# Own work tiles for the odd early stages of an RWKV layer, a new order of the stages, and two operations moved from VectorE to ScalarE

## The chip, the cores and the metric

The kernel runs on one core of one Trainium2 chip. The metric is the device time of one execution in microseconds; the time of a kernel is the median of several executions. The engines are named as the profile names them: PE is TensorE (matmuls; PEld is its weight load), DVE is VectorE, ACT is ScalarE, POOL is GpSimd, and SP is the engine whose queue issues nearly all DMA transfers.

## The reference

Two layers on a sequence of 512 tokens with 1024 features, all in float32. Layer 0 mixes tokens with RWKV-7, layer 1 with a spatial gating unit; a SwiGLU block with 2816 hidden features follows each. Every sub-layer is `x + RMSNorm(f(RMSNorm(x)))`. The part that matters here is the front of RWKV-7:

```python
xs = x[None] + xx[None] * mix[:, None, None, :]          # six mixed inputs
r, k, v = jnp.einsum('cbtd,cde->cbte', xs[:3], w_rkv)
w_raw = (w0 + jnp.tanh(xw @ w1) @ w2)
w_log = -jax.nn.softplus(-w_raw) - 0.5
decay = jnp.exp(-jnp.exp(w_log))
a = jax.nn.sigmoid(a0 + (xa @ a1) @ a2)                  # the rate
g = jax.nn.sigmoid(xg @ g1) @ g2
kk = heads(k * k_k)
kk = kk / jnp.maximum(jnp.sqrt(jnp.sum(kk * kk, axis=-1, keepdims=True)), 1e-12)
k = k * (1.0 + (a - 1.0) * k_a)
y = _rwkv7_scan(r_h, decay, k_h, v_h, -kk, kk * a_h)     # then group norm, bonus, gate, w_o
```

The scan updates a 64 x 64 state in each of 16 heads, token by token.

## The kernel before

**Tiling.** Features lie on the 128 partitions, and the 512 tokens along a row. A float32 product of full size is three matmuls of split operands (`mm3`, lines 156 to 158): each operand is split into a rounded part (`hi`, written by ScalarE, line 131) and the rest (`lo`, by VectorE, line 132). A weight comes by `weight` (line 138): a DMA into one of two `wraw` buffers, then the two halves of the split.

**Stages of the RWKV layer.** The 16 heads are worked in four groups of four heads (256 features, two slices `q` of 128), numbered b = 0 to 3. A list by hand, `PLAN` (line 33), gives the order in which the stages are written into the program:

- `P`b, `kr_proj`: the projections of k and r for the group, each copied out of PSUM by ScalarE (line 528).
- `E`b, `early`: everything for the group that works on features. From two small products it makes tanh values `tw` (decay) and `ta` (rate); a running sum `cum` of `tw` in chunks of 64 tokens; the two exponentials `Pp` and `Pi` (which overwrites `cum`); `kp`, the modified k; the sums of squares `ssp` by a matmul with a block of ones, a clamp, then Ln and Exp for the inverse root in `ri` (which overwrites `tw`); the products, and a small matmul `bps` for the bonus. At its end it stores `ma` (in `tw`'s buffer) and `r` to the DRAM tile `sa`, and `kk` and `kp` to `sb` (lines 670 to 674).
- `X0`: the mixed input for v. `V`b: the projection of v, stored to DRAM.
- `F`b, `front`: loads `MV` from `sa` and `ST` from `sb`, makes products `lm` for each of eight chunks, masks them (line 711) and copies them to `LA` and `BX`. It also clears a tile `Dm`.
- `B`b, `back`: inverts triangular blocks. It transposes `LA` into `LX` (line 734), runs a loop of small VectorE steps on `Dm`, then chains of 32 x 32 matmuls, with results in the block tile `bdT`, and updates `MV`.
- `S`b, `scan`: the chunked scan. `N`b: group norm, bonus and gate. The output projection follows.

**What sets the order.** The order of `PLAN` gives priorities. A scheduler in the tile framework, which simulates the program, then gives each engine a fixed order of instructions, in which stages are interleaved. On the chip each engine, and the SP queue, works off its list in order.

**Buffers.** Tiles of one tag share that tag's buffers, and a new tile waits until the last reader of the buffer's former tile is done, a DMA included. For `early` these are: `tw` and `ta` in tag `f0` (two buffers, line 615), `cum` and `kp` in tag `gain` (two buffers, through `gslot`, lines 625 and 636), and `k`, `r` and `Pp` in tag `e2` (seven buffers). `front` takes `Dm` from tag `f0` (line 692) and `ST` and `LA` from `e2`; `MV` and `BX` come from the general slots, which the mixed inputs of the projections use too. `bdT` (line 426) has a place of its own through the whole layer and is cleared at the start (line 427). Tag `hn` (two buffers of 128 x 1024) serves temporaries of `back`, the group norm, the bonus and the later layers.

Of the kernel before, what the change touches and what calls it, by code (L numbers as in the profile page):

```python
# [7 lines left out]
F32 = mybir.dt.float32  # L8
F32R = mybir.dt.float32r
I32 = mybir.dt.int32  # L10
AF = mybir.ActivationFunctionType
ALU = mybir.AluOpType

P = 128
T = 512
# [4 lines left out]
C = 64  # L20
# [9 lines left out]
BANKS = dict(pa=(3, 4, 0, 7), pb=(1, 2, 5, 6), h0=(1, 2, 5, 6), h1=(3, 4, 0, 7), tr=(1, 2, 5, 6))  # L30
SLOTS = 17
E2 = 7
PLAN = "P0 E0 P1 P2 E1 P3 E2 E3 X0 F0 B0 F1 V0 V1 V2 V3 B1 S0 F2 S1 F3 N0 B2 N1 B3 S2 N2 S3 N3".split()
XV = "xxxessss"
XSLOTS = 13
LAG = 2
# [46 lines left out]
class Trunk:  # L83
# [287 lines left out]
    def rwkv(self, x0, nxt):  # L371
        nc, i, tc = self.nc, self.i, self.tc
        v, a, g = nc.vector, nc.scalar, nc.gpsimd
        mm = nc.tensor.matmul
        with ExitStack() as ctx:
            ep = ctx.enter_context
            rp = ep(tc.tile_pool(name="rp", bufs=1))
# [12 lines left out]
            def e2(name, shape=(P, 2, T), dt=F32):  # L390
                return rp.tile(list(shape), dt, name=name, tag="e2", bufs=E2)
# [7 lines left out]
            def gslot(name, shape):  # L399
                return self.gp.tile(shape, F32, name=name, tag="gain", bufs=2)  # L400
# [14 lines left out]
            g.memset(bones[64:128, 64:128], 1.0)  # L415
            lnh = rp.tile([P, 1], F32, name="lnh")
            g.memset(lnh, LN_HALF)
            hsel = rp.tile([P, 2], F32, name="hsel")
            g.memset(hsel, 0.0)
            g.memset(hsel[0:64, 0:1], 0.5)  # L420
# [2 lines left out]
            g.memset(id32, 0.0)  # L423
            for r in range(0, P, 32):
                a.copy(id32[r:r + 32], self.ident[r:r + 32, r:r + 32])
            bdT = rp.tile([P, 16, 2, C], F32, name="bdT")
            g.memset(bdT, 0.0)


            w1 = s4("w1", [P, KT, 2, 64])  # L430
# [6 lines left out]
            for tt in range(TT):  # L437
                hn = e2("hn", (P, D))
# [17 lines left out]
            hka = rp.tile([P, 2, KT], F32, name="hka")  # L456
# [131 lines left out]
            def small_split(name, src_fn, b):  # L588

                raw = rp.tile([P, 2 * P], F32, name=name, tag="ss_raw", bufs=1)  # L590
                src_fn(raw, slice(b * 2 * P, (b + 1) * 2 * P))
                hi = rp.tile([P, 2 * P], F32R, name=name + "h", tag="ss_hi", bufs=2)
                lo = rp.tile([P, 2 * P], F32R, name=name + "l", tag="ss_lo", bufs=2)
                self.split(hi, lo, raw)
                return hi, lo
# [8 lines left out]
            flat = lambda t: t.rearrange("p q t -> p (q t)")  # L604
# [3 lines left out]
            def early(b, k, r):  # L608

                wh, wl = small_split("wa2", load_wa2, b)  # L610
                pc = rp.tile([P, 2, NC], F32, name="pc", tag="pc", bufs=4)
                pr = lambda q: 2 * b + q
                fcs = lambda q: slice(q * P, (q + 1) * P)

                tw, ta = (self.f0p.tile([P, 2, T], F32, name=n, tag="f0", bufs=2) for n in ("tw", "ta"))
                for q in q2:
                    acc = self.bank("pe", "w")
                    self.mm3(acc, (wh[0:64, fcs(q)], wl[0:64, fcs(q)]), (hid[0:64, 0, :], hid[0:64, 1, :]), True, True)
                    a.activation(tw[:, q, :], acc, AF.Tanh, scale=0.5, bias=halfb[:, 0, pr(q):pr(q) + 1])
                for q in q2:  # L620
                    acc = self.bank("pe", "a")
                    self.mm3(acc, (wh[64:128, fcs(q)], wl[64:128, fcs(q)]), (hid[64:128, 0, :], hid[64:128, 1, :]), True, True)
                    a.activation(ta[:, q, :], acc, AF.Tanh, scale=-0.5, bias=halfb[:, 1, pr(q):pr(q) + 1])
                v.tensor_scalar(flat(tw), flat(tw), 1.0, None, op0=ALU.add)
                cum = gslot("cum", [P, 2, T])
                for q in q2:
                    v.tensor_tensor_scan(cum[:, q], rmask.rearrange("p c t -> p (c t)"), tw[:, q], 0.0, op0=ALU.mult, op1=ALU.add)
                Pp = e2("Pp", (P, 2, NC, C + 1))
                Ppf = Pp.rearrange("p q c t -> p (q c) t")
                g.memset(Ppf[:, :, 0:1], 1.0)  # L630
                a.activation(Ppf[:, :, 1:C + 1], flat(cum).rearrange("p (c t) -> p c t", t=C), AF.Exp, scale=-DECAY)
                Pi = cum
                a.activation(flat(Pi), flat(cum), AF.Exp, scale=DECAY, bias=lnh[:, 0:1])
                v.tensor_copy(pc, Pp[:, :, :, C])

                kp = gslot("kp", [P, 2, T])
                for q in q2:
                    v.tensor_scalar(kp[:, q, :], ta[:, q, :], hka[:, 0, pr(q):pr(q) + 1], hka[:, 1, pr(q):pr(q) + 1],
                                    op0=ALU.mult, op1=ALU.add)
                v.tensor_tensor(flat(kp), flat(kp), flat(k), op=ALU.mult)  # L640

                ri = tw
                for q in q2:
                    a.activation(ri[:, q, :], k[:, q, :], AF.Square, scale=fv("rwkv_k_k", pr(q)))
                    ssp = self.bank("pe", "ssp")
                    mm(ssp, bones, ri[:, q, :], start=True, stop=True)
                    v.tensor_scalar(ri[:, q, :], ssp, 1e-24, None, op0=ALU.max)
                a.activation(flat(ri), flat(ri), AF.Ln)
                a.activation(flat(ri), flat(ri), AF.Exp, scale=-0.5)
                kk = k  # L650
                for q in q2:
                    v.scalar_tensor_tensor(kk[:, q, :], k[:, q, :], nkk[:, pr(q):pr(q) + 1], ri[:, q, :], op0=ALU.mult, op1=ALU.mult)

                sv = lambda t: flat(t).rearrange("p (c t) -> p c t", t=C)
                ma = ri
                v.tensor_tensor(sv(ma), sv(kk), Ppf[:, :, 0:C], op=ALU.mult)
                v.scalar_tensor_tensor(flat(kk), flat(ta), -1.0, flat(kk), op0=ALU.add, op1=ALU.mult)
                v.tensor_tensor(flat(kk), flat(kk), flat(Pi), op=ALU.mult)
                bps = self.bank("pe", "bps")
                for q in q2:  # L660
                    v.scalar_tensor_tensor(ta[:, q, :], r[:, q, :], fv("rwkv_r_k", pr(q)), kp[:, q, :], op0=ALU.mult, op1=ALU.mult)
                    for c in range(NC):
                        tt, par = c // 2, c % 2
                        mm(bps[par * 64:par * 64 + 64, (tt * 2 + q) * 2:(tt * 2 + q) * 2 + 2], ta[:, q, c * C:(c + 1) * C],
                           hsel, start=True, stop=True)
                BN = rp.tile([P, TT, 2, 2], F32, name="bn", tag="bn", bufs=4)
                v.tensor_copy(BN.rearrange("p t q h -> p (t q h)"), bps[:, 0:16])
                v.tensor_tensor(sv(r), sv(r), Ppf[:, :, 1:C + 1], op=ALU.mult)
                v.tensor_tensor(flat(kp), flat(kp), flat(Pi), op=ALU.mult)
                nc.sync.dma_start(out=sa[b][0], in_=ma)  # L670
                nc.sync.dma_start(out=sa[b][1], in_=r)
                for hd in range(2):
                    for n, t in ((hd, kk), (1 - hd, kp)):
                        nc.sync.dma_start(out=sb[b][head[hd], :, :, n, :].rearrange("p q c t -> p (q c) t"), in_=sv(t)[head[hd]])
                return dict(pc=pc, BN=BN)

            def front(b, o):

# [50 lines left out]
            def back(b, o):  # L729

                MV, BX, LA, Dm = (o[n] for n in ("MV", "BX", "LA", "Dm"))
                LX = e2("LX", (P, 2, 528))

                v.transpose(full(LX), LA.rearrange("p q c (x t) -> p t (q c x)", x=2))
                LAu = LA.rearrange("p q c t -> p (q c) t")

                for r in (0, 64):
                    for z, x in ((r, 0), (r + 32, 32)):
                        a.activation(LAu[z:z + 32, :, x + 16:x + 32], LAu[z:z + 32, :, x + 16:x + 32], AF.Copy,
                                     scale=mk2[z:z + 32, 0, x + 16:x + 17])  # L740
                        g.memset(LAu[z:z + 32, :, x:x + 16], 0.0)
                LXd, Dmd = diag(LX), diag(Dm)
                for j in range(15):
                    n = 15 - j
# [201 lines left out]
            xr, kr, ops, Y = None, {}, {}, {}  # L946
            for n in PLAN:
                f, b = n[0], int(n[1])
# [190 lines left out]
```

## Time and profile before

| | |
|---|---|
| median of 3 runs | 1397.12 us (1393.59 to 1397.96) |
| the profiled execution: time | 1395.72 us |
| the profiled execution: span, mean granted TensorE clock | 1394.0 us, 0.971 |
| E0 to E3, first tanh of tw starts | 60.30, 89.18, 132.32 (its second 150.48), 172.16 us |
| F0, first lm | 186.26 us |
| B0, LX | 212.87 us |
| V projections, first to last matmul | 156.7 to 263.1 us |

The span runs from the first to the last instruction; the execution's time is 1.7 us longer. Times in the trace are microseconds from the start of the span. A row of the timeline has start, duration, engine, line, operation, output and inputs, shapes, and in brackets how long the engine stood idle before it and what ended that wait. A row of one tile's or one line's instructions gives shortest, median and longest duration in ns, and the first and last start. A row of waits gives the total, the number of times and the longest.

### The profile page before, as it was taken

The page shows a single profiled execution, that of the slowest core. Times are in us where ns is not written, and L with a number is a line of the kernel's source. Part 1 is how long each engine was busy: PE and PEld are TensorE (multiplying, and loading weights), DVE is VectorE, ACT ScalarE, POOL GpSimd, SP SyncE. Part 2 cuts the span into 40 slices and gives each one's busy share as a digit, 9 for nine tenths or more (in the row PEclk, how much of TensorE's full clock was granted, in tenths as well). Part 3 has the DMA queues.
Part 4 walks back from the last instruction along what each step waited for, and adds up shares of the span by engine and source line. Part 5 has one row for each costly group of instructions (what it writes and reads, how often), then busy time and mean ns, then how long its engine had stood idle before and what let it go on. Part 6 is the DMA issues. An engine that isn't in the chain of part 4 may idle for free.

```text
span 1394.0 us, 21544 instructions
## 1 busy us (share of the span) xinstructions
PE 1332.0 (96%) x8512; PEld 1088.7 (78%) x8512; DVE 783.9 (56%) x1373; ACT 579.2 (42%) x1076; POOL 152.6 (11%) x190
## 2 busy tenths in 40 slices
PE   5999979989799899999999999999999999999998
PEld 3677768878687688888888887878888888888886
DVE  7975776579847565544553225575574554453223
ACT  5665765566543453222322224543463332232121
POOL 5000200111000021111110002010121111110000
PEclk8999979989799999999999999999999999999999
DMA  5145375432214233333322332342223333332231
GB/s 150 36 140 148 108 208 166 127 77 69 92 49 158 61 101 112 91 95 102 91 91 91 103 109 76 107 138 89 91 77 93 103 91 93 103 92 91 91 105 61
DMA packets 209956, 142.00 MB, mean 102 GB/s; under 512 B 59536, under 2 KB 185024, under 8 KB 209856
## 3 DMA queue, kind: packets, MB, share of 16 engines
q1 hardware_dynamic: 208560, 135.91, 33.0%
q0 software_dynamic: 1296, 4.72, 1.0%
q8 instruction: 67, 1.10, 0.3%
q14 instruction: 33, 0.27, 0.1%
HBM read 124.35 MB, written 14.16 MB: 99 GB/s over the span
## 4 chain that ended last, share of the span: by engine, by line
PE 62%; DVE 2%; ACT 0%; issue 0%; DVEq 0%
PE gu L157 12%; PE gu L158 12%; PE gu L156 11%; PE acc L157 8%; PE acc L158 8%; PE acc L156 8%; PE u L158 1%; PE u L157 1%; PE u L156 1%; DVE x L273 1%; PE s L1065 1%; PE ptr L218 0%; DVE hT L59 0%; DVE rt L208 0%; DVE ry L209 0%; DVE hn L270 0%
## 5 line engine op out<-in xcount | busy, mean ns | idle before, releaser
L131 ACT CAST whi<-wraw 128x1024 fp32r<-128x1024 f32 x177 | 185.7, 1049 | 481.3 <-PE gu L157 250.5
L132 DVE TENSOR_TENSOR wlo<-wraw,whi 128x1024 fp32r<-128x1024 f32 x177 | 263.1, 1487 | 206.3 <-ACT whi L131 202.3
L156 PE MATMUL gu<-hT,whi 128*128 128x512 f32 (+1 forms) x768 | 288.8, 378 | 1.8 <-ACT hT L57 1.7
L157 PE MATMUL gu<-hT,whi 128*128 128x512 f32 (+1 forms) x768 | 288.5, 377 | 1.1 <-DVE hT L59 1.1
L158 PE MATMUL gu<-hT,wlo 128*128 128x512 f32 (+1 forms) x768 | 289.5, 378 | 0.0
L156 PEld LDWEIGHTS gu<-hT,whi 128*128 128x128 f32 x768 | 145.0, 190 | 31.5 <-ACT hT L57 2.3
L157 PEld LDWEIGHTS gu<-hT,whi 128*128 128x128 f32 x768 | 144.9, 189 | 30.5 <-DVE hT L59 1.5
L158 PEld LDWEIGHTS gu<-hT,wlo 128*128 128x128 f32 x768 | 145.1, 189 | 28.5 <-issue 0.2
L157 PE MATMUL acc<-wlo,act 128*128 128x512 f32 x416 | 164.0, 394 | 0.0
L156 PE MATMUL acc<-whi,act 128*128 128x512 f32 x416 | 163.5, 394 | 0.0
L158 PE MATMUL acc<-whi,act 128*128 128x512 f32 x416 | 160.4, 394 | 0.0
L332 DVE TENSOR_TENSOR sg<-sg,gu 128x512 f32<-128x512 f32 x44 | 30.3, 688 | 142.2 <-PE gu L158 139.2
L333 POOL TENSOR_TENSOR sg<-sg,hn 128x512 f32<-128x512 f32 x44 | 57.0, 1295 | 417.3 <-DVE sg L332 417.3
L156 PEld LDWEIGHTS acc<-whi,act 128*128 128x128 f32 x416 | 78.2, 188 | 18.1
L158 PEld LDWEIGHTS acc<-whi,act 128*128 128x128 f32 x416 | 78.2, 188 | 18.0
L157 PEld LDWEIGHTS acc<-wlo,act 128*128 128x128 f32 x416 | 78.1, 188 | 18.0
L330 DVE TENSOR_TENSOR sg<-gu,hn 128x512 f32<-128x512 f32 x44 | 30.4, 691 | 66.5 <-PE gu L158 66.3
L131 ACT CAST act<-sg 128x512 fp32r<-128x512 f32 x52 | 32.3, 621 | 71.7 <-POOL sg L333 57.5
L156 PE MATMUL proj<-xsp,whi 128*128 128x512 f32 x128 | 51.6, 403 | 0.0
L158 PE MATMUL proj<-xsp,wlo 128*128 128x512 f32 x128 | 51.1, 401 | 0.0
L157 PE MATMUL proj<-xsp,whi 128*128 128x512 f32 x128 | 50.3, 396 | 0.2 <-DVE xsp L132 0.2
L708 PE MATMUL lm<-MV,ST 128*128 128x128 f32 x256 | 40.0, 309 | 7.0 <-ACT BX L726 3.0
(303 smaller groups left out, 2124.0 us busy)
## 6 DMA issues: line engine op xcount, KB each, us to landing
wraw<-in_ffn_w_gate_dram SPq DMA_DIRECT2D x44, 512.0 KB
wraw<-in_ffn_w_up_dram SPq DMA_DIRECT2D x44, 512.0 KB, 3.8
wraw<-in_ffn_w_down_dram SPq DMA_DIRECT2D x44, 512.0 KB, 3.7
wraw<-in_rwkv_w_rkv_dram SPq DMA_DIRECT2D x24, 512.0 KB, 3.7
wraw<-in_sgu_w_in_dram SPq DMA_DIRECT2D x16, 512.0 KB, 3.7
x<-in_x_dram SPq DMA_DIRECT2D x8, 512.0 KB, 3.2
MV<-sa SPq DMA_DIRECT2D x64, 64.0 KB, 2.5
ST<-sb SPq DMA_DIRECT2D x8, 512.0 KB
```

Of the source, the lines that this page charges most:

```text
L131: self.nc.scalar.copy(hi, src)
L132: self.nc.vector.tensor_tensor(lo, src, hi.bitcast(F32), op=ALU.subtract)
L156: mm(out, lhs[0], rhs[0], start=start, stop=False)
L157: mm(out, lhs[0], rhs[1], start=False, stop=False)
L158: mm(out, lhs[1], rhs[0], start=False, stop=stop)
L273: v.scalar_tensor_tensor(xts[tt][:, c], f, y[:, 0:1], xts[tt][:, c], op0=ALU.mult, op1=ALU.add)
L330: nc.vector.tensor_tensor(sg, pp[0], yb, op=ALU.mult)
L332: nc.vector.tensor_tensor(sg, sg, pp[1], op=ALU.mult)
L333: nc.gpsimd.tensor_tensor(sg, sg, yb, op=ALU.mult)
L708: mm(lm[:, cc * P:(cc + 1) * P], st[:, cc].rearrange("p n t -> p (n t)"), mv[:, :, cc, hd, :], start=True, stop=True)
L1065: mm(acc[:, tt * P:(tt + 1) * P], vt[tt][:, m * P:(m + 1) * P], wsT[:, m, :], start=True, stop=True)
```

## The change

E1 and E3 take `tw` and `ta` from one new tile `tws` in a tag `bd`, and `cum` and `kp` from `hn`; E0 and E2 keep theirs. `bdT` becomes a tile of the same tag `bd` (one buffer), made and cleared when the first `back` is written. In `PLAN`, `E1` moves ahead of `P2` and `E2` ahead of `P3`. The affine form of the rate (line 638) becomes an Identity activation on ScalarE. The clamp of the sums of squares at 1e-24 (line 647, a maximum on VectorE) becomes a Relu of the sum minus 1e-24 on ScalarE, and Ln adds 1e-24 again; a tile `tiny` holds the two constants.

```diff
-PLAN = "P0 E0 P1 P2 E1 P3 E2 E3 X0 F0 B0 F1 V0 V1 V2 V3 B1 S0 F2 S1 F3 N0 B2 N1 B3 S2 N2 S3 N3".split()
+PLAN = "P0 E0 P1 E1 P2 E2 P3 E3 X0 F0 B0 F1 V0 V1 V2 V3 B1 S0 F2 S1 F3 N0 B2 N1 B3 S2 N2 S3 N3".split()
...
+            tiny = rp.tile([P, 2], F32, name="tiny")
+            g.memset(tiny[:, 0:1], -1e-24)
+            g.memset(tiny[:, 1:2], 1e-24)
...
-            bdT = rp.tile([P, 16, 2, C], F32, name="bdT")
-            g.memset(bdT, 0.0)
+            bd = lambda name, shape: rp.tile(shape, F32, name=name, tag="bd", bufs=1)
...
-                tw, ta = (self.f0p.tile([P, 2, T], F32, name=n, tag="f0", bufs=2) for n in ("tw", "ta"))
+                if b % 2:
+                    tws = bd("tws", [P, 2, 2, T])
+                    tw, ta = tws[:, 0], tws[:, 1]
+                    room = lambda name: self.sm.tile([P, 2, T], F32, name=name, tag="hn", bufs=2)
+                else:
+                    tw, ta = (self.f0p.tile([P, 2, T], F32, name=n, tag="f0", bufs=2) for n in ("tw", "ta"))
+                    room = lambda name: gslot(name, [P, 2, T])
...
-                cum = gslot("cum", [P, 2, T])
+                cum = room("cum")
...
-                kp = gslot("kp", [P, 2, T])
+                kp = room("kp")
                 for q in q2:
-                    v.tensor_scalar(kp[:, q, :], ta[:, q, :], hka[:, 0, pr(q):pr(q) + 1], hka[:, 1, pr(q):pr(q) + 1],
-                                    op0=ALU.mult, op1=ALU.add)
+                    a.activation(kp[:, q, :], ta[:, q, :], AF.Identity, scale=hka[:, 0, pr(q):pr(q) + 1],
+                                 bias=hka[:, 1, pr(q):pr(q) + 1])
...
-                    v.tensor_scalar(ri[:, q, :], ssp, 1e-24, None, op0=ALU.max)
-                a.activation(flat(ri), flat(ri), AF.Ln)
+                    a.activation(ri[:, q, :], ssp, AF.Relu, bias=tiny[:, 0:1])
+                a.activation(flat(ri), flat(ri), AF.Ln, bias=tiny[:, 1:2])
...
+            inv = []
...
             def back(b, o):
+                if not inv:
+                    inv.append(bd("bdT", [P, 16, 2, C]))
+                    g.memset(inv[0], 0.0)
+                bdT = inv[0]
```

## The prediction

> **What bounds the kernel now.** I read the page first: busy shares, the clock line and the chain that ended last.
> ```profile
> span 1394.0 us, 21544 instructions
> PE 1332.0 (96%) x8512; PEld 1088.7 (78%) x8512; DVE 783.9 (56%) x1373; ACT 579.2 (42%) x1076; POOL 152.6 (11%) x190
> PEclk8999979989799999999999999999999999999999
> PE 62%; DVE 2%; ACT 0%; issue 0%; DVEq 0%
> ```
> TensorE is busy for 96% of the span, and the chain at the end is its own matmuls. The granted clock drops below nine tenths only in the first eleven of forty slices, that is, in the RWKV layer. So the kernel is limited by TensorE, and what can be won are two things in that layer: TensorE's idle time and its time at a low clock. Second view: busy time by stretches cut at the ends of the early stages E and the first front stage F0.
> ```profile
> 100.00:156.00 56.00, 56.00 (x258) 42.16 (x257) 34.30 (x41) 30.70 (x41) 6.85 (x15) 1.00 0.47 136
> 156.00:172.00 16.00, 16.00 (x113) 13.50 (x111) 11.94 (x17) 11.37 (x15) 1.75 (x4) 1.00 0.34 89
> 172.00:186.00 14.00, 12.75 (x89) 11.08 (x88) 8.04 (x11) 8.33 (x11) 1.04 (x2) 0.76 0.86 203
> 186.00:207.00 21.00, 13.46 (x104) 11.74 (x103) 17.93 (x24) 15.03 (x35) 2.23 (x4) 0.81 0.71 196
> 207.00:240.00 33.00, 32.78 (x518) 32.07 (x521) 24.36 (x50) 18.55 (x43) 3.38 (x8) 0.91 0.58 175
> 240.00:264.00 24.00, 21.08 (x308) 20.17 (x295) 7.11 (x12) 8.77 (x20) 1.56 (x3) 0.86 0.27 76
> 264.00:300.00 36.00, 31.18 (x636) 27.52 (x636) 26.24 (x65) 24.96 (x68) 7.42 (x17) 0.93 0.52 134
> 340.00:390.00 50.00, 41.14 (x663) 34.25 (x664) 41.70 (x91) 26.56 (x57) 1.22 (x4) 0.80 0.28 85
> ```
> The columns are length, busy us of PE, PEld, DVE, ACT and POOL, then clock and DMA. From 100 to 172 TensorE is full at full clock: nothing moved inside that stretch can win time there. The hole is 186 to 207: 7.54 us idle at clock 0.81. Third view: the order of time around it and the waits, to see who makes the hole.
> ```profile
> 158.02 0.58 ACT L528 COPY r<-proj 128x512 f32<-128x512 f32 x1
> 172.16 1.27 ACT L619 ACTIVATE tw<-w,halfb 128x512 f32<-128x512 f32 x2 [4.56 <-DMA sa<-tw]
> 186.26 1.95 PE L708 MATMUL lm<-MV,ST 128*128 128x128 f32 x16
> 192.91 3.75 PE L708 MATMUL lm<-MV,ST 128*128 128x128 f32 x16 [3.04 <-ACT BX L726]
> 196.95 0.33 SPq L670 DMA_DIRECT2D sa<-tw  x1
> 197.81 1.64 SPq L138 DMA_DIRECT2D wraw<-in_rwkv_w_rkv_dram  x2
> 206.96 0.58 PE L157 MATMUL v<-wlo,xsp 128*128 128x256 f32 x1 [1.02 <-DVE wlo L132]
> 203.84 1.22 DVE L669 TENSOR_TENSOR kp<-kp,cum 128x1024 f32<-128x1024 f32 x1
> 212.87 2.05 DVE L734 STREAM_TRANSPOSE LX<-LA 128x1024 f32<-128x1024 f32 x1 [0.77 <-ACT LA L714]
> ...
> POOL LA L694 <- DMA sa<-r: 28.8, 2, 23.7
> POOL Dm L695 <- DMA sa<-tw: 17.2, 1, 17.2
> ACT tw L619 <- DMA sa<-tw: 4.6, 1, 4.6
> ```
> E3's last input, r, is evicted at 158.02, but E3's first tanh starts at 172.16: it writes tw, whose buffer E2 gives back only when its store of tw has landed. All four early stages share the two f0 buffers (tw, ta) and the two gain buffers (cum, kp), so they cannot overlap. E3 therefore ends with its kp product at 203.84, in the middle of F0. Three things follow. F0's Dm needs an f0 buffer and waits 17.2 us for E3's store; F0's LA needs a buffer of E2's k, r or Pp and waits for the store of r; and on the in-order SP queue the next two weights of the V projections are issued at 197.81, behind E3's store at 196.95, so that TensorE's filler returns only at 206.96. Between, TensorE waits for ScalarE and VectorE, which do E3 and F0 together.
>
> **The change, part by part.** (1) Buffers. E1 and E3 get tws (tag bd) and two hn buffers; E0 and E2 keep f0 and gain. E3 then waits for E1's release only, not for E2's. F0's Dm takes an f0 buffer that E2 gave back, so the 17.2 us wait goes. (2) Order. E1 moves ahead of P2 and E2 ahead of P3. Their tensor work moves within the full stretch that ends at 172, so it displaces projections one for one: 0 there. The covering work on the other engines has room: from 100 to 156 DVE is busy 34.30 of 56 and ACT 30.70. If that cover were gone, the stretch would grow by what exceeds 56, and nothing I move comes near it. E1's and E2's stores go ahead of later weights on SP in this stretch as well; TensorE is full there, and a store is issued in 0.33 us. After the change only the part of E3 that needs k and r is left behind P3. Before, E3 took from 172.16 to 205.06, 32.9 us. The tensor work of E2 and E3 that now comes ahead delays P3's end by an allowance of 7 us: three times the 4 x 0.59 us of ssp in a stage (row below), my estimate. Started without a wait at 158.02 + 7 and with the same 32.9 us, E3 ends at 198 at the latest; with its tanh, scan and Exp done under P3, what is left is the stretch from Ln to the end, 187.19 to 205.06, and it ends near 183. F0 begins when E2's k, r and Pp are stored and the projections' slots come free, about 165 instead of 186.26. So LX and the back stage B0 come some 20 us sooner.
>
> (3) The two operations that change engine.
> ```profile
> L619 ACT ACTIVATE tw<-w,halfb x8: 681/690/696, 60.3 to 172.7; 128x512 f32<-128x512 f32 x8
> L644 ACT ACTIVATE tw<-k,vecT x8: 706/724/730, 72.1 to 181.6; 128x512 f32<-128x512 f32 x8
> L647 DVE TENSOR_SCALAR tw<-ssp x8: 683/686/692, 77.7 to 186.5; 128x512 f32<-128x512 f32 x8
> L646 PE MATMUL ssp<-tw,bones x16: 590/592/595, 75.5 to 185.8; 128*128 128x512 f32 x16
> L638 DVE TENSOR_SCALAR kp<-ta,hka x8: 527/546/549, 72.8 to 188.6; 128x512 f32<-128x512 f32 x8
> ...
> 182.22 1.13 ACT L633 ACTIVATE cum<-cum,lnh 128x1024 f32<-128x1024 f32 x1
> 184.21 1.28 ACT L648 ACT_TABLE_LOAD   x1
> 187.19 1.06 ACT L648 ACTIVATE tw<-tw 128x1024 f32<-128x1024 f32 x1 [1.70 <-DVE tw L647]
> ```
> VectorE loses 8 x 0.546 and 8 x 0.686: 9.9 us, 2.5 a stage. ScalarE gains eight Identity passes, taken as L644 (scale from a tile): 5.8 us; eight Relu passes out of PSUM with a bias from a tile, taken as L619: 5.5 us; and a bias on Ln, as L633 has it, 1.13 against 1.06: 0.3 us. That is 11.6 us, 2.9 a stage. Inside a stage the chain loses a crossing between engines and gains a table load: at 184.21 it hid behind the wait for VectorE, and behind a Relu on the same engine it cannot. From -0.6 to +1.28 us a stage; E3 alone is near the path, and its end has some 10 us of slack against F0, so 0. Behind the new instructions on ScalarE stand the casts of weights.
>
> (4) bdT shares tws's buffer.
> ```profile
> 3.27 1.81 POOL L427 MEMSET bdT<- 128x2048 f32 x1
> 240.47 0.68 DVE L786 COPY bdT<-Tp 32x512 f32<-32x512 f32 x1 [1.67 <-PE Tp L781]
> ```
> Its memset of 1.81 us moves to the start of B0 and must wait for E3's last reader. Its first user stood at 240.47, and 20 us sooner it is still 20 us behind E3's latest end: 0. Were that gone, Dm's memset of F1, queued behind it on POOL, would wait as well. The two small memsets at the start cost POOL nothing that anyone waits for.
>
> **The sum.** What the hole costs is idle time plus clock loss (one minus the clock, times busy time). 172 to 186: 1.25 + 3.06. 186 to 207: 7.54 + 2.56. 207 to 240: 0.22 + 2.95. Together 17.6 us. The losses from 240 to 264 are B0's own and stay. I do not expect all of it, because E3 and F0 still overlap somewhat; one stall of the present kind is left in.
> ```profile
> 173.40 0.63 PE L664 MATMUL bps<-hsel,ta 128*64 128x2 f32 x16 [1.25 <-DVE ta L661]
> 174.42 0.28 PE L156 MATMUL v<-whi,xsp 128*128 128x256 f32 x1
> 174.54 0.28 PE L157 MATMUL v<-wlo,xsp 128*128 128x256 f32 x1
> 175.70 0.41 PE L156 MATMUL v<-whi,xsp 128*128 128x256 f32 x1
> 175.91 0.41 PE L157 MATMUL v<-wlo,xsp 128*128 128x256 f32 x1
> 182.06 0.28 PE L156 MATMUL v<-whi,xsp 128*128 128x256 f32 x1
> ```
> After a wait of 1.25 us the same matmuls come every 0.21 us instead of 0.12, from about 175.7 to 182.06: 6.4 x (1 - 0.12/0.21) = 2.7 us, so a stall costs 4.0 us. 17.6 - 4.0 = 13.6 us less. The profiled execution took 1395.72 us, which gives 1382.1; it was 1.4 us under the median of 1397.12, so I predict 1384 us for the median, and 1378 to 1390 for this case.
>
> **The rivals.** (a) Slower: ScalarE becomes the bound between 145 and 185. It would do E2's end, all of E3, the casts for the last projections and V, and F0's copies. From 156 to 207 it was busy 11.37 + 8.33 + 15.03 = 34.7 of 51 us; compressed into 40 us with 3 to 6 us of new passes it is at 95 to 100%. The casts then come late and TensorE stalls at 4.0 us each. Five stalls instead of the one that I left in eat the gain, and six give 17.6 - 24.0, or 6.4 us more than now: 1404 us. Against it: E2 leaves the window. The Trainium skill, ScalarE: Activation LUTs, Rules for kernel authors, speaks for this rival: it puts relu, max and multiply on VectorE. By it this case, 1404 us, would be the forecast. The trace agrees for the affine form (0.546 on VectorE against 0.72) and not for the clamp (0.686 against 0.69). (b) Given back: the V projections are used up sooner as filler, and B0 and the first scan run with less beside them. The stretch from 340 to 390, which has no such filler, loses 8.9 idle and 8.2 by the clock, a third of its time; 40 us of that give back 13 of the 13.6 us: 1396 us. Also here is that the change does not do what it says: the scheduler that orders the engines leaves E3 as late as it was, the sum is then 0, and the time 1397. (c) The clock does not recover. If it is the small matmuls of F0 and B0 and not the waits that lower it, only 1.25 + 7.54 + 0.22 = 9.0 us can go, 7.8 with one wait left: 1389 us. The Trainium skill, TensorE: Matmul & The Clock Gate, What's actually happening, lets the clock fall after an idle window of some 3.4 us. By it none of the waits above, the longest 3.04 us, would lower the clock, and the sum would be this rival's; the trace shows the slow matmuls 2 us behind a wait of 1.25 us, so I give it little. (d) More: the earlier F1 and B1 also fill the holes from 240 to 264 (2.92 + 2.95) and part of 264 to 300 (4.82 + 2.18): 25 us or so, 1371 us.
>
> **How the numbers follow.** Forecast 0.40, (c) 0.13, (d) 0.10, (b) 0.19, (a) 0.18. Under 0.3% (4.2 us) a measurement of this kernel cannot be told from no change. The first three are faster, with 0.04 of (b): 0.67; most of (b) is the same: 0.14; slower takes (a) and 0.01 of (b): 0.19. The range leaves out the far side of (d) and two thirds of (a): 1370 to 1400.
>
> **What would show it.** Right: E3's first tanh does not wait for sa<-tw; F0's Dm memset has no long wait; LX of B0 starts before 198; TensorE is over 19 of 21 us busy between 186 and 207, and its clock is above 0.9 from 172 to 240. Wrong: casts L131 that start late with ScalarE full before them (a); V's last matmul much earlier with new idle time behind it (b); a full TensorE at a clock near 0.8 (c); or TensorE idle before 156.

## The result and the profile after

The changed kernel took 1404.94 us (median; 1404.03 to 1408.17), the one before, beside it, 1396.59 us: a ratio of 1.0066 (95% interval 1.0048 to 1.0085). It is slower by 8.3 us, where 13 us less was forecast. The page of the changed kernel, its span, busy times and granted clock:

```profile
span 1406.4 us, 21550 instructions
PE 1331.7 (95%) x8512; PEld 1086.6 (77%) x8512; DVE 775.7 (55%) x1357; ACT 588.6 (42%) x1092; POOL 153.5 (11%) x192
PEclk9999997999799999999999999999999999999999
```

TensorE does the same work (1331.7 us busy, 1332.0 before) in a longer span, and the low clock still lies in the first eleven slices. The last matmul of the RWKV layer's output projection starts at 484.01 us before and at 496.14 after; what comes behind it takes 910 us in both. So nearly all of the loss is inside that layer. (This profile is of the slowest of the four executions, 1408.17 us; e14 below profiles another one, of 1402.67 us.) Since TensorE's busy time is the same, the 12.4 us by which the span is longer are idle time of TensorE, and 10.1 us of them lie between 172 and 390 us. The stretches of the prediction, in the changed kernel (length, busy us of PE, PEld, DVE, ACT, POOL, clock, DMA):

```profile
172.00:186.00 14.00, 12.46 (x103) 11.88 (x102) 10.84 (x13) 13.07 (x23) 0.85 (x2) 1.00 0.42 109
186.00:207.00 21.00, 17.14 (x164) 15.85 (x163) 12.73 (x23) 12.34 (x34) 4.07 (x7) 1.00 0.63 142
207.00:240.00 33.00, 24.39 (x457) 23.00 (x459) 18.29 (x34) 12.64 (x26) 1.12 (x2) 0.79 0.56 176
240.00:264.00 24.00, 20.84 (x276) 20.25 (x268) 7.11 (x12) 7.48 (x17) 0.90 (x2) 0.86 0.22 62
264.00:300.00 36.00, 31.06 (x422) 26.76 (x421) 27.24 (x67) 26.16 (x74) 8.16 (x20) 1.00 0.57 145
300.00:340.00 40.00, 32.77 (x545) 28.53 (x547) 31.69 (x80) 18.12 (x42) 5.30 (x12) 0.87 0.21 53
340.00:390.00 50.00, 42.06 (x694) 34.93 (x689) 35.75 (x88) 31.50 (x76) 1.62 (x6) 0.83 0.26 78
```

The hole from 186 to 207 is smaller, as forecast: 17.14 us busy at full clock, 13.46 at 0.81 before. But 207 to 240, where TensorE was full (32.78 of 33), is now a hole of 8.61 us. By the prediction's own measure (idle time, and one minus the clock times the busy time), 172 to 264 lost 23.5 us before and 25.2 after. From 264 to 390 the loss rose too, from 28.0 to 31.5. For this the row of 300 to 340 of the kernel before is needed as well:

```profile
300.00:340.00 40.00, 38.45 (x398) 33.42 (x393) 34.63 (x93) 26.56 (x72) 5.79 (x14) 0.94 0.29 74
```

The timeline of the changed kernel shows the order of events:

```profile
151.71 0.69 ACT L628 ACTIVATE tws<-w,halfb 128x512 f32<-128x512 f32 x1
173.12 1.13 PE L720 MATMUL lm<-MV,ST 128*128 128x128 f32 x8
190.00 1.21 DVE L679 TENSOR_TENSOR kp<-kp,cum 128x1024 f32<-128x1024 f32 x1
202.70 1.97 DVE L750 STREAM_TRANSPOSE LX<-LA 128x1024 f32<-128x1024 f32 x1 [1.78 <-ACT LA L726]
214.00 0.68 DVE L723 TENSOR_TENSOR MV<-lm,mk 64x512 f32<-64x512 f32 x1 [6.09 <-PE lm L720]
227.99 2.09 DVE L769 STREAM_TRANSPOSE Dt<-Dm 128x1024 f32<-128x1024 f32 x1
...
195.04 10.65 SPq L701 DMA_DIRECT2D MV<-sa  x14
206.45 1.22 SPq L694 DMA_DIRECT2D ST<-sb  x2
209.66 2.35 SPq L138 DMA_DIRECT2D wraw<-in_rwkv_w_rkv_dram  x2
211.85 3.40 PE L720 MATMUL lm<-MV,ST 128*128 128x128 f32 x16 [6.75 <-DMA ST<-sb]
...
312.53 1.95 DVE L750 STREAM_TRANSPOSE LX<-LA 128x1024 f32<-128x1024 f32 x1
315.10 0.69 DVE L821 COPY bdT<-T2p 32x512 f32<-32x512 f32 x1
```

Read it from the top. E3 starts at 151.71 without a wait for a store and F0's Dm is cleared at 152.37, long before anyone needs it; E3 ends at 190.00 + 1.21 instead of 205.06; F0 begins at 173.12 instead of 186.26 (the prediction had 165; SP issues F0's MV loads only from 167.97 on); B0's LX comes at 202.70 instead of 212.87. Then B0's loop on VectorE stops, from 207.9 to 214.00: inside it, in VectorE's fixed order, stands a mask of F1 (line 723), which waits for lm, which waits 6.75 us for F1's ST. That load was issued at 206.45, behind 14 of F1's MV loads, which occupied SP for 10.65 us. V's next weights are issued behind it, at 209.66. So V's matmuls are missing too; the first two rows below are of the kernel before, the next two of the changed one (shortest, median, longest ns; first and last start):

```profile
L158 PE MATMUL v<-whi,xsp x23: 277/282/416, 169.8 to 184.4; 128*128 128x256 f32 x23
L156 PE MATMUL v<-whi,xsp x55: 276/283/415, 203.6 to 237.9; 128*128 128x256 f32 x55
```

```profile
L156 PE MATMUL v<-whi,xsp x51: 276/283/682, 169.5 to 198.7; 128*128 128x256 f32 x51
L156 PE MATMUL v<-whi,xsp x32: 276/283/581, 219.1 to 235.8; 128*128 128x256 f32 x32
```

Before, V had a gap from 184.4 to 203.6; now it has one from 198.7 to 219.1. The hole was not filled, it was moved with the filler. F1's MV loads stood ahead of V's weights in the kernel before as well, 11 us sooner:

```profile
183.82 9.88 SPq L689 DMA_DIRECT2D MV<-sa  x15
```

The weights behind them were issued at 197.81. The prediction named E3's store of 196.95 as what these weights stood behind; SP spent 0.33 us on that store and had waited 1.2 us for its input, against 9.88 us on the MV loads. In the changed kernel the same loads start later, and the weights with them. And further on, LX of B2 (312.53) now stands ahead of the last bdT copy of B1 (315.10; 307.55 before, where LX of B2 followed at 314.57).

### The profile page after: what moved, and what is told of

The parts are those of the page before. It is cut to its first block, busy times and chain, and to the rows that moved or that the text cites. A ratio compares the mean times of both kernels' runs of the same rounds, so it can differ in the third digit from the quotient of the medians.

```text
span 1406.4 us, 21550 instructions
## 1 busy us (share of the span) xinstructions
PE 1331.7 (95%) x8512; PEld 1086.6 (77%) x8512; DVE 775.7 (55%) x1357; ACT 588.6 (42%) x1092; POOL 153.5 (11%) x192
## 4 chain that ended last, share of the span: by engine, by line
PE 61%; DVE 2%; ACT 0%; issue 0%; DVEq 0%
PE gu L157 11%; PE gu L156 11%; PE gu L158 11%; PE acc L158 8%; PE acc L157 8%; PE acc L156 8%; PE u L157 1%; PE u L158 1%; PE u L156 1%; DVE x L273 1%; PE s L1081 1%; DVE hT L59 0%; PE ptr L218 0%; DVE rt L208 0%; DVE ry L209 0%; DVE hn L270 0%
```

## The experiments

Two theories. **The order:** none of the three parts costs by itself; every change of the work makes the scheduler write new fixed orders for all engines, and in them loads of F1, weights and group norms stand ahead of B0's and B1's chains. **The engine move:** ScalarE's new passes are the price. A third suspect was the sharing of buffers.

**One part alone (e1, e2, e3), and two of three (e4, e5).**

```diff
# e1: kernel before, and only
-  v.tensor_scalar(kp[:, q, :], ta[:, q, :], hka..., hka..., op0=ALU.mult, op1=ALU.add)
+  a.activation(kp[:, q, :], ta[:, q, :], AF.Identity, scale=hka..., bias=hka...)
-  v.tensor_scalar(ri[:, q, :], ssp, 1e-24, None, op0=ALU.max)
+  a.activation(ri[:, q, :], ssp, AF.Relu, bias=tiny[:, 0:1])     # and Ln with a bias
# e2: kernel before, and only the buffers tws, hn, bd for E1 and E3, and bdT in bd
# e3: kernel before, and only
-PLAN = "P0 E0 P1 P2 E1 P3 E2 E3 ...
+PLAN = "P0 E0 P1 E1 P2 E2 P3 E3 ...
# e4: e2 and e3 together (the changed kernel without e1's part)
# e5: e1 and e2 together (the changed kernel with the old PLAN)
```

> Only the two operations moved to ScalarE; buffers and order of the stages as before. Theory A (the parts cost nothing by themselves; the loss of 9 us comes from the order in which the scheduler then places F1 inside B0, and later N0 and B2 ahead of B1): E3 still ends near 205 us and the time stays within 4 us of before. Rival B (the move to ScalarE is the price: 9.5 us more ScalarE work and a table load that is no longer hidden): slower by 5 to 12 us.

> Only the buffers: tws and hn for E1 and E3, bdT in the shared tag; order of the stages and VectorE operations as before. Theory A: E3's first tanh comes earlier than 172 us; the time depends on where F1 then falls, anything from -8 to +10 us, with a wait of lm on the load of ST if it is slower. Rival C (sharing hn and bdT's place costs by waits on these buffers): slower by 5 us or more, with waits that name kp, cum, hn or bdT.

> Only the order of the stages: E1 ahead of P2, E2 ahead of P3; shared buffers and VectorE operations as before. Theory A: E1 and E2 end earlier, E3 can start when E2's store has landed, about 150 to 160 us; the gain or loss is of the same size as in the full change, and the sign is the scheduler's. Rival D (the order alone is the loss, since E1's and E2's matmuls displace projections): slower by about 9 us with P3's end near 165 us.

> The full change without the move to ScalarE. Theory A: E3 ends near 190 us as in the full change; the time may fall on either side of before. Rival B: the 9 us come back, 1396 us or less, and lm does not wait for ST.

> The change with the old order of the stages: buffers and ScalarE operations. If the scheduler's new arrangement of the later stages is what costs, and any edit of the engines' work brings one on: 1398 to 1407 us, with the loss between 207 and 365 us of the span and not in the early stages. If ScalarE's two operations are the price: 1406 us, like the kernel with them alone (1.0074), and the casts L131 late. If buffers make room for the operations (less waiting of E stages for each other): 1394 to 1398 us.

| kernel | median us | ratio to before (95%) |
|---|---|---|
| e1, operations | 1406.37 | 1.0074 (1.0049 to 1.0100) |
| e2, buffers | 1395.61 | 0.9996 (0.9974 to 1.0018) |
| e3, order | 1406.30 | 1.0061 (1.0041 to 1.0082) |
| e4, buffers and order | 1405.88 | 1.0070 (1.0046 to 1.0094) |
| e5, buffers and operations | 1401.33 | 1.0033 (1.0010 to 1.0056) |
| the whole change | 1404.94 | 1.0066 (1.0048 to 1.0085) |

Against what was written down: e1 came out as the theory of the engine move had it (5 to 12 us slower), with E3's end at 211.0 and not near 205. e2 came out as the theory of the order had it: E3's first tanh at 166.50, the time unchanged. e3 met the number of the rival that blames the delay of P3 (P3 ends near 165; it was 163.86), but e15 below has P3's end at 162.86 and is the fastest kernel here. e4 missed the engine move's forecast on both counts: it is slower, and lm waits 2.8 us for ST. e5 lies in the order's range (1398 to 1407 us), but its loss is not where that theory put it: from 207 to 365 us TensorE was 143.03 us busy at a clock of 0.90, and 142.77 at 0.89 before.

The parts do not add. The sharing of buffers is free, and the engine move is not the sole price, since e4 loses as much without it. The operations cost 10 us alone and nothing on top of buffers and order (1404.94 against 1405.88). Where they cost, TensorE's waits from 172 to 264 us show how (total, times, longest), in e1:

```profile
PE bkt L724 <- ACT BX L718: 5.6, 3, 3.4
```

With the old order and shared buffers E3 and F0 are on ScalarE at once, F0's BX copies come late, and LX of B0 slips from 212.87 to 224.6. The buffers and the order pull E3 and F0 apart. The new order alone brings LX at 201.5 and still loses: e3 has the wait of lm for ST too (2.2 us), as e4 has.

**F1 behind V3 (e6, e7, e8).** If F1's loads and masks in the wrong place are the hole, F1 has to go later:

```diff
-PLAN = "P0 E0 P1 E1 P2 E2 P3 E3 X0 F0 B0 F1 V0 V1 V2 V3 B1 ...
+PLAN = "P0 E0 P1 E1 P2 E2 P3 E3 X0 F0 B0 V0 V1 V2 V3 F1 B1 ...
# e6: the changed kernel with this; e7: the kernel before with F1 moved alike
# e8: e6 with the two operations back on VectorE
```

> The changed kernel with F1 written behind V3 in the order of the stages (X0 F0 B0 V0 V1 V2 V3 F1 B1), nothing else. If the lead of B0 is lost because F1's loads and masks stand inside B0's loop on VectorE and ahead of V's weights on SP: the wait of lm for ST near 212 us goes, the loop of B0 runs through, Dt of B0 is written before 223 us (228.0 in the changed kernel, 231.8 in the one before), TensorE is over 31 of 33 us busy between 207 and 240, and the time is 1386 to 1397 us. If the lead cannot be kept whatever the order, because the later stages give it back: 1402 to 1407 us, with 207 to 240 filled and the loss later, since F1 and B1 come later. If ScalarE's new work is the price: 1402 to 1407 us.

> The kernel before with the same move of F1 behind V3 and nothing else of the change. If F1's place is a fault that only the early end of E3 brings out: 1396 to 1406 us, since here B0's loop was hardly cut before. If F1 behind V3 is better by itself, whatever the change does: 1385 to 1393 us, as much gain as in the changed kernel.

> The changed kernel with F1 behind V3 and the two operations back on VectorE: buffers and order of stages alone. If ScalarE's work costs nothing by itself: within 4 us of the kernel with F1 late and the operations on ScalarE. If it is a price of its own: 6 to 10 us less than that kernel. If VectorE was the bound of the loop in B0: 2 to 6 us more.

e6: 1398.72 us, 1.0019 (1.0000 to 1.0037). e7: 1396.54, 1.0003 (0.9985 to 1.0021). e8: 1392.72, 0.9974 (0.9945 to 1.0002). F1's place was worth 6 us in the changed kernel, 13 us in e4 (against e8), and nothing in the one before, as the theory of the order asks. In e6 SP issues V's two weights ahead of ten of F1's MV loads, which follow at 197.88, and V's gap is 4 us long instead of 20:

```profile
194.79 3.04 SPq L138 DMA_DIRECT2D wraw<-in_rwkv_w_rkv_dram  x2
L156 PE MATMUL v<-whi,xsp x50: 276/283/369, 169.8 to 198.3; 128*128 128x256 f32 x50
L156 PE MATMUL v<-whi,xsp x59: 276/283/415, 202.4 to 231.1; 128*128 128x256 f32 x59
```

The time of this issue tells the runs apart. The first of these V weights is issued at 209.66 in the changed kernel (208.82 in e14), 210.39 in e1, 212.66 in e3 and 210.41 in e4, the four that are 0.6 to 0.7% slower than the kernel before. In all other runs it is issued at 199.4 or sooner. Of those only e12 and, by 0.3%, e5 are clearly slower than the kernel before, so their loss lies elsewhere.

e8 is 6.0 us under e6, the low end of what was written down for a price of the operations' own (6 to 10 us); this comes up again below. In e6 the wait for ST is gone and 207 to 240 is 28.19 us busy, not the 31 that was expected; Dt of B0 came at 225.30, no earlier than 223, and the time is 1.7 us above the written range (1386 to 1397). Its timeline shows the next thing in the way:

```profile
216.09 9.04 SPq L847 DMA_DIRECT2D su<-Vd  x8
227.77 1.04 SPq L138 DMA_DIRECT2D wraw<-in_rwkv_w_o_dram  x2
234.44 1.22 DVE L132 TENSOR_TENSOR wlo<-wraw,whi 128x1024 fp32r<-128x1024 f32 x1 [6.86 <-ACT whi L131]
235.59 0.68 DVE L788 TENSOR_TENSOR Qs<-Qp,id 128x512 f32<-128x512 f32 x1
```

Qs is the first step of B0's triangular chain. Its input was there (Dt and Qp were done by 228.3), but on VectorE it stands behind wlo, half of a weight of the output projection, which is needed 150 us later; that weight was issued on SP behind eight su loads, which read what V stores.

**The late weight (e9 to e12).**

```diff
# e9 (on e6), e11 (on e8), e12 (on the kernel before): its second half on GpSimd
-  hi, lo = self.weight(wrows(u)[:, :, cols[half]], spare=own)
+  hi, lo = self.weight(wrows(u)[:, :, cols[half]], spare=own, pool=bool(spare) and not half)
# e10 (on e6): only its load, by GpSimd's queue instead of SP's
+  hi, lo = self.weight(wrows(u)[:, :, cols[half]], spare=own, q=nc.gpsimd if spare and not half else None)
```

> The changed kernel with F1 late, and the second half of the split of the output projection's first weights (wlo) on GpSimd instead of VectorE: VectorE's order is otherwise as in the kernel with F1 late. There Qs, the first step of B0's triangular chain, stood 6.86 us behind a wlo whose weight landed late. If that queue is what the changed kernel with F1 late loses against the one with the operations on VectorE: Qs starts before 230 us instead of 235.59, TensorE's wait for Qs (4.8 us) goes, bdT of B0 comes near 235 instead of 240, and the time is 1391 to 1396 us. If ScalarE's operations cost it elsewhere: 1397 to 1400 us, with Qs early all the same. If the clock then takes the lead away between 340 and 400 us: 1396 to 1399 us, with B2's bdT before 362 us.

> The same kernel with F1 late, and only the loads of the output projection's first weights issued by GpSimd's queue instead of SP's; no engine's order is changed. If SP's order (eight su loads and two stores of V ahead of the weight, issued at 227.77 us) made the weight late: it lands before 228 us, Qs starts before 231 us, and the time is 1391 to 1396 us. If the weight waits for its buffer and not for SP: nothing changes, 1397 to 1400 us.

> The changed kernel with F1 late, the two operations on VectorE and wlo of the output projection's first weights on GpSimd. If each of the three places found (F1's, the operations', the weight's) has its own price and these add: 1388 to 1392 us. If the new arrangement that the edit brings, or the clock in the later stages, decides: 1392 to 1402 us.

> The kernel before with wlo of the output projection's first weights on GpSimd, nothing else. Before, the chain of B0 did not wait for such a weight for long. If moving wlo away is worth something only where the weight stands before Qs: 1394 to 1402 us. If it relieves VectorE in any case: 1388 to 1393 us.

e9: 1395.17 us, 0.9991 (0.9965 to 1.0017). e10: 1395.81, 0.9987 (0.9969 to 1.0006). e11: 1394.15, 0.9979 (0.9961 to 0.9997). e12: 1409.40, 1.0094 (1.0061 to 1.0127). In e10 no engine's order changed, the weight was issued at 216.68, and Qs came 5 us sooner; the medians of e9 and e10 are about 3 us under e6, though the intervals overlap. On e8 the edit of e9 makes new orders and brings nothing that shows (e11; 1388 to 1392 us were written down for prices that add). The timeline of e10:

```profile
210.06 0.55 SPq L138 DMA_DIRECT2D wraw<-in_rwkv_w_rkv_dram  x1
214.06 1.05 ACT L131 CAST whi<-wraw 128x1024 fp32r<-128x1024 f32 x1 [1.68 <-DMA wraw<-in_rwkv_w_rkv_dram]
215.14 1.22 DVE L132 TENSOR_TENSOR wlo<-wraw,whi 128x1024 fp32r<-128x1024 f32 x1 [2.95 <-ACT whi L131]
216.68 0.93 POOL L138 DMA_DIRECT2D wraw<-in_rwkv_w_o_dram  x1 [6.93 <-DVE Dm L765]
227.30 1.98 DVE L769 STREAM_TRANSPOSE Dt<-Dm 128x1024 f32<-128x1024 f32 x1
230.56 0.69 DVE L788 TENSOR_TENSOR Qs<-Qp,id 128x512 f32<-128x512 f32 x1
```

e12 missed all its expectations: one kind of instruction taken off VectorE in the kernel before made it 12 us slower. Its Qs even came sooner (234.2 against 235.0), and its last bdT of B3 came 11.9 us later (419.58 against 407.69). GpSimd needs 2.39 us for such a wlo and VectorE 1.22, but that is not the loss: from 200 to 500 us TensorE waits only 0.5 us for a wlo. That leaves the new order as the likeliest cause; which of the moved instructions does it I did not trace, so it is not shown.

**What one execution adds (e13, e14, e16), and the last wait (e15, e17).** e13 is the kernel before, e14 the changed one and e16 e9, unchanged and profiled again. e15 is e8, e17 the kernel before, each with e10's load by GpSimd's queue:

```diff
+  (q or nc.sync).dma_start(out=raw, in_=src)          # in weight(); q=nc.gpsimd as in e10
```

> The kernel before, unchanged, profiled once more, to see what of a stage's loss belongs to the order of the instructions and what to one execution. If the order sets TensorE's idle time and its clock alike: between 172 and 264 us again about 11.9 us idle and 12.1 lost by the clock, between 320 and 400 about 10.1 and 7.7, each within 1 us. If the clock after a short wait is a matter of the execution: the idle times within 1.5 us, the clock's losses 3 to 6 us apart in some stage.

> The changed kernel, unchanged, profiled once more. The hole between 207 and 240 us must show again if it is the order's: lm waits 6 to 7 us for ST near 212, 24 to 25 us busy of 33. If it was an accident of that execution: over 28 us busy. The clock's losses may differ by 3 to 6 us in a stage if they are the execution's.

> The kernel with F1 late and wlo on GpSimd, unchanged, profiled once more (its first profile had a span of 1388.7 us, its median was 1395.2). If the clock is the execution's: idle time within 1.5 us of the first profile in each stage, span 1390 to 1400 us, and the difference in the clock's losses. If the first profile is typical of the order: span 1388 to 1390 us.

> F1 late, the two operations on VectorE, and the output projection's first weights loaded by GpSimd's queue: the order of every other engine as in the kernel with F1 late and the operations on VectorE (1392.7 us, 0.9974). If the late weight costs there too (2.62 us of VectorE's wait ahead of Qs): 1389 to 1392 us. If the lead of B0 is given back to TensorE's low clock between 340 and 400 us: 1392 to 1396 us, with B2's bdT before 360 us and B3's near 406.

> The kernel before with only the loads of the output projection's first weights issued by GpSimd's queue; no engine's order is changed. If a late weight costs only where it stands ahead of B0's chain, which the early stages' change brought about: 1393 to 1398 us, ratio 0.997 to 1.002. If that queue is better whatever the early stages do, and the 0.9941 is its doing: 1386 to 1391 us.

The three took 1393.94, 1402.67 and 1390.73 us, one execution each. The hole of the changed kernel shows again in e14 (6.0 us of lm waiting for ST; 24.22 of 33 us busy): it belongs to the order. In e16 the span is 1389.0 us as in e9's first profile (1388.7); e9's ten executions took 1388.04 to 1404.92 us, so two profiles at the fast end do not show what is typical of its order. The clock is partly the execution's. e13, stretch and timeline:

```profile
172.00:186.00 14.00, 12.06 (x105) 9.88 (x105) 9.46 (x13) 9.27 (x12) 1.04 (x2) 1.00 0.85 199
```

```profile
173.69 0.63 PE L664 MATMUL bps<-hsel,ta 128*64 128x2 f32 x16 [1.24 <-DVE ta L661]
```

The same wait, 1.24 us here and 1.25 in the first profile, was followed by a clock of 1.00 here and of 0.76 there. Together 172 to 264 lost 20.3 us in e13 against 23.5, and the idle time alone 14.2 against 11.9: it varied more than I had expected.

e15 took 1387.77 us, a ratio of 0.9941 (0.9921 to 0.9960): faster than both kernels. e17 took 1394.55, 0.9986 (0.9972 to 0.9999), so the queue alone gives little, and F1's late place alone gave nothing (e7). The two together without the early stages' new buffers and order were not run, so how much of e15's gain needs those is not shown. The stretches of e15 and part of its timeline:

```profile
172.00:186.00 14.00, 13.29 (x133) 12.66 (x132) 13.56 (x18) 6.54 (x15) 1.35 (x1) 1.00 0.55 129
186.00:207.00 21.00, 17.20 (x134) 16.72 (x134) 7.78 (x11) 12.96 (x34) 5.66 (x11) 0.92 0.76 206
207.00:240.00 33.00, 30.17 (x580) 29.53 (x579) 21.02 (x44) 13.28 (x25) 4.72 (x9) 0.91 0.69 167
240.00:264.00 24.00, 21.54 (x234) 19.05 (x234) 14.76 (x33) 18.58 (x49) 5.37 (x12) 0.98 0.52 159
```

```profile
206.28 2.06 DVE L747 STREAM_TRANSPOSE LX<-LA 128x1024 f32<-128x1024 f32 x1 [0.74 <-ACT LA L723]
206.81 0.55 SPq L138 DMA_DIRECT2D wraw<-in_rwkv_w_rkv_dram  x1
212.68 1.23 DVE L132 TENSOR_TENSOR wlo<-wraw,whi 128x1024 fp32r<-128x1024 f32 x1 [0.45 <-ACT whi L131]
223.33 2.01 DVE L766 STREAM_TRANSPOSE Dt<-Dm 128x1024 f32<-128x1024 f32 x1
```

172 to 264 now loses 14.3 us: 9 less than the kernel before in its first profile, 6 less than in its second. Against e10, which differs by the operations on ScalarE and is 6 to 8 us slower (6.4 by the ratios, 0.9987 against 0.9941; 8.0 by the medians), LX starts at the same 206.3, but Dt is 4.0 us sooner. In e10 the wlo of a V weight inside B0's loop waits 2.95 us, since SP issued that weight at 210.06 instead of 206.81; ScalarE was idle and waiting for it. So in this pair, too, the price of the operations begins with a place in a queue and not with a full ScalarE. The rest of the pair I have not traced.

Six pairs of runs differ by the operations alone. With them on ScalarE the kernel is slower by 0.74% (e1 against the kernel before), 0.37% (e5, e2), 0.45% (e6, e8), 0.12% (e9, e11) and 0.46% (e10, e15), and equal in one pair (the changed kernel, e4). So a price of the operations' own is not refuted. New orders come with each of these edits, and how much of the price is the passes' and how much the orders' stays open.

## Why the prediction was wrong

What held: E3 starts without a wait; its end at 191.2 lies in 183 to 198; the allowance for P3 (7 us) measured 7.6 (P3's last copy of r starts at 165.64 instead of 158.02); bdT's memset, done by 191.9, was waited for by nobody. The moved operations, from the changed kernel:

```profile
L647 ACT ACTIVATE kp<-ta,hka x4: 812/816/827, 71.8 to 137.0; 128x512 f32<-128x512 f32 x4
L657 ACT ACTIVATE tw<-ssp,tiny x4: 693/698/702, 79.9 to 137.7; 128x512 f32<-128x512 f32 x4
```

The Relu costs the 0.69 us that was taken, the Identity 0.82 instead of 0.72. Weighing both the same way as before: against VectorE's 0.546 the affine form is the worse on ScalarE, as the Trainium skill (ScalarE: Activation LUTs, Rules for kernel authors) has it, and the clamp is equal.

What failed, in order of weight:

- **The sum's first step: the losses of 172 to 186, 186 to 207 and 207 to 240, "Together 17.6 us", go but for one stall.** It took the hole as something that goes when E3 ends earlier, since it read V's weights as held by E3's store. The hole is a gap of the filler V, and what held V's weights in SP's queue were mostly F1's MV loads: 9.88 us before, 10.65 us after, where they stood ahead of F1's ST too. I counted the stores that go ahead of weights on SP while TensorE is full, and not the next stage's loads. F0 began at 173.12 and not near 165, LX came 10 us sooner, not 20, TensorE was 17.14 and not over 19 of 21 us busy, and 8.61 us of idle time came back from 207 to 240, where 0.22 had been.
- **"The losses from 240 to 264 are B0's own and stay", and nothing said of what comes later.** 264 to 390 lost 31.5 us instead of 28.0 (33.3 in e14). The lead was not only given back, as rival (b) has it; B1 fell behind. The rows of 312.53 and 315.10 show one such place: a transposition of B2 ahead of B1's last copy.
- **The price of a stall, 4.0 us, and the clock's part of the hole.** e13 shows that the 3.06 us of 172 to 186 were one execution's. The Trainium skill, TensorE: Matmul & The Clock Gate, What's actually happening, says that the window over which activity is judged runs freely; the two profiles with the same wait and clocks of 0.76 and 1.00 are compatible with that, and I had weighed only the length of the idle window.
- **The rivals.** The time, 1404, is that of rival (a), but not its mechanism, so the agreement is luck: ScalarE was 13.07 of 14 us busy between 172 and 186, with TensorE at full clock and 1.54 us idle. In e1, where the operations stand alone, TensorE does wait for ScalarE (5.6 us of bkt for the BX copies), which comes near to it. A rival was missing: that the scheduler's new orders cost as much as the change gains.

How far the gain was there to be had, by the starts of the transposition Dt in B0, of VectorE's copy of bdT from T2p in B1, B2 and B3, and of the output projection's last matmul:

| us | Dt B0 | bdT B1 | bdT B2 | bdT B3 | last matmul |
|---|---|---|---|---|---|
| before (e13) | 231.84 | 307.55 (305.44) | 369.60 (367.24) | 407.69 (407.76) | 484.01 (482.74) |
| after | 227.99 | 315.10 | 375.19 | 420.11 | 496.14 |
| e10 | 227.30 | 295.86 | 360.60 | 408.04 | 484.32 |
| e15 | 223.33 | 292.52 | 357.64 | 403.58 | 478.65 |

Against the two profiles of the kernel before, e10 and e15 lead by 7 to 15 us at B1 and B2, and between B2 and B3 lose 5 to 9 of it. That part of rival (b), the lead given back, is right. Part of it is the clock: e8 and the kernel before do the same step, with the same kind of wait ahead of it, e8 first:

```profile
396.96 0.26 PE L794 MATMUL Tp<-Dt,Qs 32*32 32x32 f32 x7 [1.74 <-issue]
397.08 1.77 PE L805 MATMUL Q2p<-Dn,LA 32*32 32x32 f32 x64
```

```profile
401.28 0.26 PE L781 MATMUL Tp<-Dt,Qs 32*32 32x32 f32 x8 [1.84 <-issue]
401.42 1.20 PE L792 MATMUL Q2p<-Dn,LA 32*32 32x32 f32 x64
```

64 equal matmuls take 1.77 us in the one and 1.20 in the other. How much of the lead goes this way and how much by TensorE simply having less filler stays open.

## What to carry to other kernels

A hole in a full engine is a gap in its filler: before counting it as won, follow the filler's loads through the DMA queue, and list what the earlier stage will now put ahead of them, its DMAs first. Where a scheduler writes the engines' orders, an edit's own price can be smaller than that of the new orders (e1 to e5, e7 and e12 moved the time by 0 to +0.9%, though in e1 and e5 part of it may be the operations' own), so read the place of prefetched weights and of the next stage's masks in the in-order queues of the critical loop, and mend those; a queue that leaves every engine's order alone is the cheapest tool for it (worth 0.1 to 0.3% here). Take the clock's loss after short waits from two profiles, not from one.

## What the runs showed of the hardware

A wait of 1.2 us was followed by a clock loss of 3.06 us in one execution of a program and by none in another (the kernel before and e13, 172 to 186). Executions of e15 spread from 1382.43 to 1394.87 us, and the granted clock goes broadly with them: 0.983 in the two lowest, 0.973 in the highest. And the SP queue, which the profile's page does not list among the busy engines, set when V's weights and F1's ST were issued: 14 MV loads took it 10.65 us, 0.76 us each with the gaps between them, and eight su loads 9.04 us, waits included.
